# A gated delta-rule recurrence cut into one stream per head pair, each with its own PSUM bank, and emitted in an order that counts more time for VectorE's steps

## The chip, the core and the metric

The kernel runs on one core of one Trainium2 chip. The metric is the device time of one execution in microseconds (us). The engines are named as the profile names them: PE is TensorE (PEld its weight loads), DVE is VectorE, ACT is ScalarE, POOL is GpSimd and SP the engine that issues the DMAs. Each engine works through its own instructions strictly in the order in which they were emitted.

## What is computed

One layer of a hybrid streaming encoder for 2048 prompt rows and 32 sample rows of width 1024: a LayerNorm, one wide input projection, a chunk-band softmax attention (branch A), a gated DeltaNet (branch B), two output projections, a gated merge and a last projection with LayerNorm. Branch B has 8 heads of width 64 and works on chunks of 64 rows. Its core, cut to what matters here, is a scan over the chunks:

```python
def step(s, blk_in):
    q_c, k_c, u_c, w_c, gc_c, qk_c = blk_in
    v_new = u_c - jnp.einsum('bhld,bhde->bhle', w_c, s)
    o_c = (jnp.einsum('bhld,bhde->bhle', q_c * jnp.exp(gc_c)[..., None], s)
           + jnp.einsum('bhij,bhje->bhie', qk_c, v_new))
    g_last = gc_c[..., -1]
    k_dec = k_c * jnp.exp(g_last[..., None] - gc_c)[..., None]
    s = s * jnp.exp(g_last)[..., None, None] + jnp.einsum('bhld,bhle->bhde', k_dec, v_new)
    return s, o_c
s_final, o = lax.scan(step, s0.astype(f32), (qb, kb, u, w, gc, qk))
```

The state `s` of a chunk is needed by the next chunk of the same head, and by no other head.

## The kernel before

The prompt is worked on in two halves of 1024 rows. Each half has a stage for branch B (`phase_b`, here called the first and the second recurrence stage) and one for branch A (`phase_a`); after the second attention stage the branches are merged. The input projections are not a stage of their own. `fetch`, `divide` and `multiply` stream the 49 weight blocks through all stages, and their products (tile `pj`, three f16 passes that stand for one f32 product) are what PE does between the small products of the stage. Which jobs a stage gets is fixed (`ORDER`, `FILL`, `TAIL`): in a recurrence stage they are the blocks of branch B and some gate blocks, and the jobs of the attention stage can begin only when the recurrence stage has ended (`done`), since its buffers take the same memory.

Nothing is scheduled by the tile framework. Python generators emit the instructions: `Flow.run` always steps the generator whose clock is earliest, `Engine.price` puts a cost on each instruction, and `Flow.spend` moves the generator's clock to the end that these costs give. So these clocks are a plan, from which nothing but the order on each engine is left. A `Gate` hands out slots (buffers), a `Mark` is an event.

In a recurrence stage the 8 heads are 4 pairs (`p` 0 to 3, two heads side by side on the 128 partitions), and a half has two blocks of 8 chunks for each pair; the second half ends with one block for the sample rows. For each block `prep` makes the decays, `local`/`system` the chunk products (`k_bd`, `qk_bd`), `solve`/`substitute` the triangular systems on DVE (`sys_t`, `sys_u`), `side` the scaled operands (`q_bd`, `kd_bd`, `v_t`), and `inverse` assembles `u_bd` from the solved parts (`tu`, `z_c`). Then `chain` runs the recurrence over the block, and `tail` normalises its rows (`v_t`), transposes them on PE and stores them.

`chain` (L1255 on) is one generator for all blocks in a row. A chunk has five f32 products of 64 columns, each done in two passes, and four small steps: `xs` = state by `k_bd` (PE), `os` = state by `q_bd` (PE), `r` (DVE, reads `xs`), `ys` = `r` by `u_bd` (PE), `vn` (DVE, reads `ys`), `ds` = `vn` by `kd_bd` (PE), `os` += `vn` by `qk_bd` (PE), the new state (DVE, reads `ds`), and a copy of `os` to `v_t` (ACT). `xs`, `os` and `ys` take turns in three PSUM banks (`a`), `ds` has one of its own (`c`); `a` serves `inverse` and `tail` as well.

```python
yield bank["a"]
xs = pt("a")
PE.matmul(xs[:, 0:HD], k.kb[:, c, :], st, start=True, stop=True)
yield bank["a"]
os_ = pt("a")
PE.matmul(os_[:, 0:HD], k.qb[:, c, :], st, start=True, stop=False)
```

The line number of nearly every instruction in the profile is that of the helper that emits it (L243), so operations are told by their tiles.

Of the kernel before, what the change touches and what calls it, by code (L numbers as in the profile page):

```python
# [11 lines left out]
F32 = mybir.dt.float32  # L12
# [37 lines left out]
HEAD, TAIL = [2, 3], [6, 6]  # L50
AHEAD = 100.0
SPREAD = 20.0
HOP_PE, HOP, HOP_SAME = 0.1, 0.2, 0.12
# [28 lines left out]
class Gate:  # L82
# [169 lines left out]
def trunk(ctx: ExitStack, tc: tile.TileContext, x_p, x_s, cache_k, cache_v, st_conv, st_gdn,  # L252
# [11 lines left out]
    def dma(dst, src, eng=nc.sync):  # L264

        eng.dma_start(dst, src)  # L266
        n = 4
        for k in dst.shape:
            n *= k

        n = max(n, n // (4 * dst.shape[-1]) * 768)
        return flow.transfer("SP" if eng is nc.sync else "S", n)

    def gate(n):
        return Gate(flow, n)

    def mark():
        return Mark(flow)
# [4 lines left out]

    banks = {"pj": 2, "a": 3, "b": 2, "c": 1}
    bank = {k: gate(n) for k, n in banks.items()}

    def pt(tag):

        return psum.tile([P, 512], F32, tag=tag, bufs=banks[tag], name=tag)

# [448 lines left out]
    def phase_b(half):  # L739

        stack = ExitStack()
        bp = stack.enter_context(tc.tile_pool(name=f"bp{half}", bufs=1, reuse_waits="tile"))
        last = half == 1
# [26 lines left out]

        pd = [dram.tile([32, 1024], F32, name=f"sol_p{half}{i}") for i in range(NSIDE)]
        ud = [dram.tile([32, 1024], F32, name=f"sol_u{half}{i}") for i in range(NSIDE)]

# [39 lines left out]
        raw_slots, qk_slots, v_slots = gate(2), gate(NQK), gate(2)  # L813
        par_slots, side_slots, u_slots = gate(NPAR), gate(NSIDE), gate(NSIDE)
        e_slot, tail_slot, p_slots, vt_slots = gate(1), gate(2), gate(NSIDE), gate(NSIDE)
        todo, decays, q_sys = Queue(flow), Queue(flow), Queue(flow)
# [176 lines left out]
        def prep():  # L993
            yield decay_done
            for k in order:
# [23 lines left out]
                yield  # L1019
                k.sc = bp.tile([P, 4, 8], F32, tag="sc", bufs=7, name="sc")  # L1020
                s_k, s_l = (k.sc[:, i, 0:nch] for i in (2, 3))
# [45 lines left out]
        def side(k, ss):  # L1067
# [4 lines left out]
            G.tensor_tensor(out=k.sc[:, 0, 0:nch], in0=ss[:, 1, 0:nch], in1=expo[:, 1, 0:nch], op=ALU.pow)  # L1072
            yield side_slots
            k.qb, k.kdb = q_bd[k.n % NSIDE], kd_bd[k.n % NSIDE]
            for h in range(2):
# [25 lines left out]
            yield from by_token(k.qk[:, 1, :], nch, put_k)  # L1101
            yield vt_slots
            k.v_t = bp.tile([P, 8, HD], F32, tag="v_t", bufs=NSIDE, name="v_t")
            yield bank["b"]
# [16 lines left out]
        def system(k):  # L1121

            nch = k.nch
            n = nch * CH
            yield par_slots
            yield k.qk_ready
            yield k.prep
            yield p_slots
            kb, qkb = k.kb, k.qkb = k_bd[k.n % NPAR], qk_bd[k.n % NPAR]
            p_c = k.p_c = bp.tile([P, 8, HD], F32, tag="p_c", bufs=NSIDE, name="p_c")  # L1130
# [4 lines left out]
            ss = bp.tile([P, 2, 8], F32, tag="ss", bufs=6, name="ss")  # L1135
            k.rr = bp.tile([P, 8], F32, tag="rr", bufs=7, name="rr")
            yield bank["b"]
# [26 lines left out]

            dv = pd[k.n % NSIDE][:].rearrange("(c k) (j i) -> k j c i", k=4, i=32)
            for q in range(4):
# [5 lines left out]
        def solve():  # L1172
            while True:
                k, t = yield from q_sys.get()
                sys_p = bp.tile([P, 32, 32], F32, tag="sys_p", bufs=2, name="sys_p")
                sys_u = bp.tile([P, 8, 32], F32, tag="sys_u", bufs=2, name="sys_u")
                sys_t = bp.tile([P, 8, 32], F32, tag="sys_t", bufs=2, name="sys_t")
                G.memset(sys_u[:], 0.0)
                for g in range(4):
                    G.memset(sys_u[g * 32:(g + 1) * 32].rearrange("p r i -> p (r i)")[:, g::36], 1.0)  # L1180
                yield t
                p0 = pd[k.n % NSIDE][:]
                yield dma(sys_p[:].rearrange("p j i -> p (j i)"),
                          bass.AP(p0.tensor, p0.offset, [[0, 4], [1024, 32], [1, 1024]]))
                yield from substitute(sys_p, sys_u, sys_t)
                for g in range(4):
                    t = dma(ud[k.n % NSIDE][:].rearrange("s (r g i) -> g s r i", g=4, i=32)[g], sys_u[g * 32:(g + 1) * 32])
                flow.start(inverse(k, t))
# [15 lines left out]
        def inverse(k, t):  # L1204

            yield u_slots
            k.ub = u_bd[k.n % NSIDE]
            nch, ub, p_c = k.nch, k.ub, k.p_c
            u0 = ud[k.n % NSIDE][:]
            yield t  # L1210
# [33 lines left out]
            for h in range(2):  # L1244
# [3 lines left out]
                bank["ba"[h]].give()  # L1248
            p_slots.give()
            yield k.side  # L1250
            k.ready.done()


        def chain():
            for k in order:  # L1255
                yield k.ready
                sc, v_t = k.sc, k.v_t
                for c in range(k.nch):
                    st = k.state[c]
                    vc = v_t[:, c if k.p is None else c % 4 * 2 + c // 4, :]  # L1260
                    yield bank["a"]
                    xs = pt("a")
                    PE.matmul(xs[:, 0:HD], k.kb[:, c, :], st, start=True, stop=True)
                    yield bank["a"]
                    os_ = pt("a")
                    PE.matmul(os_[:, 0:HD], k.qb[:, c, :], st, start=True, stop=False)
                    flow.cur.last = None
                    r = bp.tile([P, HD], F32, tag="r", bufs=2, name="r")
                    V.scalar_tensor_tensor(out=r[:], in0=xs[:, 0:HD], scalar=k.negc[:, c:c + 1],
                                           in1=vc, op0=ALU.mult, op1=ALU.add)  # L1270
                    bank["a"].give()
                    yield bank["a"]
                    ys = pt("a")
                    PE.matmul(ys[:, 0:HD], k.ub[:, c, :], r[:], start=True, stop=True)
                    yield
                    vn = bp.tile([P, HD], F32, tag="vn", bufs=2, name="vn")
                    V.tensor_scalar(out=vn[:], in0=ys[:, 0:HD], scalar1=sc[:, 1, c:c + 1], scalar2=None, op0=ALU.mult)
                    bank["a"].give()
                    yield
                    yield bank["c"]  # L1280
                    ds_ = pt("c")
                    PE.matmul(ds_[:, 0:HD], k.kdb[:, c, :], vn[:], start=True, stop=True)
                    PE.matmul(os_[:, 0:HD], k.qkb[:, c, :], vn[:], start=False, stop=True)
                    V.scalar_tensor_tensor(out=st, in0=st, scalar=sc[:, 3, c:c + 1], in1=ds_[:, 0:HD],
                                           op0=ALU.mult, op1=ALU.add)
                    bank["c"].give()

                    S.copy(out=vc, in_=os_[:, 0:HD])
                    bank["a"].give()
                    yield  # L1290
                for g in (par_slots, side_slots, u_slots):
                    g.give()
                flow.start(tail(k))

        def tail(k):
# [43 lines left out]
            else:  # L1339
# [20 lines left out]
                yield t  # L1360
            vt_slots.give()
            if k.p is None:
# [3 lines left out]
            tail_slot.give()  # L1366
            if k is order[-1]:
                done.done()
# [5 lines left out]

        for g in (worker(todo), worker(decays), prep(), local(), solve(), solve(), chain()):
            flow.start(g)
        return stack, make, done


    def phase_a(half):  # L1380
        stack = ExitStack()
        ap = stack.enter_context(tc.tile_pool(name=f"ap{half}", bufs=1, reuse_waits="tile"))
        last = half == 1
# [756 lines left out]

    with tc.tile_pool(name="x0", bufs=1, reuse_waits="tile") as xp:
# [87 lines left out]
```

## Time and profile before

| what | us |
|---|---|
| median of 3 runs (lowest to highest) | 2184.65 (2179.92 to 2190.05) |
| the profiled execution | 2182.41 |
| its span in the profile | 2180.4 |
| PE busy | 2014.9 |
| DVE busy | 1563.9 |
| ACT busy | 1024.8 |
| POOL busy | 636.1 |
| first recurrence stage, about | 47 to 559 |
| first attention stage, about | 559 to 888 |
| second recurrence stage, about | 888 to 1410 |
| second attention stage, about | 1410 to 1795 |
| merge, about | 1795 to 2180 |

A row of instructions names the engine, the operation, the tile written and the tiles read, and the shape. In the table of groups the numbers after the bar are busy us and mean ns of one, and after the second bar the engine's idle us just before these instructions, with the instruction that ended most of it. In the table of windows each engine has its busy us and its number of instructions; PEclk is the granted share of PE's clock. In the timeline a row has its start, its length and, in brackets, the idle time before it and what ended that.

### The profile page before, as it was taken

The numbers are of one execution on the slowest core, as the hardware profiler recorded it, in microseconds if no ns is written. First come the engines' busy times: TensorE is split into PE (matmuls) and PEld (weight loads), VectorE is DVE, ScalarE is ACT, GpSimd is POOL, SyncE is SP. The second block draws the span as 40 slices with busy tenths as digits, with TensorE's granted clock in tenths as the row PEclk, the third lists the DMA queues.
The fourth block names the chain that finished last, engine by engine and source line by source line (L and its number), as shares of the span: only waits on it lengthen the run. The fifth ranks groups of instructions, "written<-read, shape, count | busy, mean of one in ns | idle before, by whom it ended". The sixth has DMA issues, their size and how long they took to land. (4 is left out here: it accounts for less than half of the span.)

```text
span 2180.4 us, 41182 instructions
## 1 busy us (share of the span) xinstructions
PE 2014.9 (92%) x15098; PEld 1441.5 (66%) x15098; DVE 1563.9 (72%) x4700; ACT 1024.8 (47%) x2178; POOL 636.1 (29%) x708
## 2 busy tenths in 40 slices
PE   4898998999899999998999999889999998999998
PEld 4454665666455556666777776667676577998896
DVE  7689878873378677679898877447567577676675
ACT  5654545433476677564443533256666652111110
POOL 6343333232212113333223332310110214443333
PEclk9999999999899999999999999999999999999999
DMA  3233232322213113222223223221221325443331
GB/s 119 71 83 104 76 93 53 90 86 83 72 47 102 47 62 111 66 66 66 72 63 98 66 85 89 85 82 41 70 64 47 117 86 192 135 133 110 116 104 59
DMA packets 181718, 185.99 MB, mean 85 GB/s; under 512 B 73862, under 2 KB 131570, under 8 KB 181516
## 3 DMA queue, kind: packets, MB, share of 16 engines
q1 hardware_dynamic: 181516, 183.36, 28.1%
q8 instruction: 119, 1.95, 0.4%
q14 instruction: 83, 0.68, 0.1%
HBM read 135.91 MB, written 50.53 MB: 86 GB/s over the span
## 5 line engine op out<-in xcount | busy, mean ns | idle before, releaser
L243 PE MATMUL pj<-hi,whi 128*128 128x512 f16 (+2 forms) x1992 | 660.1, 346 | 25.6 <-DVE ql L243 7.4
L243 PE MATMUL pj<-hi,wlo 128*128 128x512 f16 (+2 forms) x1952 | 649.8, 345 | 0.9 <-POOL wlo L243 0.9
L243 PEld LDWEIGHTS <-whi 128*128 128x128 f16 x3984 | 412.7, 105 | 230.8 <-issue 17.9
L243 PE MATMUL pj<-lo,whi 128*128 128x512 f16 (+2 forms) x1992 | 458.6, 342 | 0.0
L243 POOL TENSOR_TENSOR wlo<-wraw,whi 128x512 f16<-128x512 f32 x192 | 228.3, 1190 | 702.3 <-ACT whi L243 454.1
L243 PEld LDWEIGHTS <-wlo 128*128 128x128 f16 x1952 | 205.0, 105 | 124.1 <-issue 24.5
L243 ACT CAST mh<-sg 128x256 fp32r<-128x256 f32 x64 | 26.0, 406 | 283.0 <-DVE sg L243 283.0
L243 DVE TENSOR_TENSOR sys_u<-sys_u,sys_t 128x60 f32<-128x60 f32 (+24 forms) x527 | 135.8, 258 | 18.5 <-DVE sys_t L243 0.2
L243 PE MATMUL a<-ghi,whi 128*128 128x256 f32 (+1 forms) x512 | 133.6, 291 | 7.2 <-DVE sg L243 6.9
L243 ACT ACTIVATE wraw<-wraw,w_scale 128x1024 f32<-128x1024 f32 (+1 forms) x98 | 111.4, 1137 | 56.8 <-DVE w_scale L243 56.3
L243 ACT CAST ph<-b 128x512 f16<-128x512 f32 (+2 forms) x224 | 92.4, 421 | 88.2 <-PE b L243 81.5
L243 PE MATMUL a<-ghi,wlo 128*128 128x256 f32 (+1 forms) x512 | 131.8, 288 | 1.0 <-DVE wlo L243 0.9
L243 ACT CAST whi<-wraw 128x512 f16<-128x512 f32 (+1 forms) x196 | 119.6, 611 | 20.2 <-PE pj L243 17.2
L243 ACT ACTIVATE sb<-sb,mx,unit 128x640 f32<-128x640 f32 (+4 forms) x128 | 109.0, 852 | 39.6 <-DVE mx L243 38.8
L243 DVE TENSOR_TENSOR pl<-b,ph 128x512 f16<-128x512 f32 (+2 forms) x224 | 107.2, 485 | 24.1 <-ACT ph L243 22.9
L243 DVE TENSOR_TENSOR sys_t<-sys_u,sys_p 128x60 f32<-128x60 f32 (+21 forms) x459 | 116.3, 253 | 4.7
L243 ACT COPY v_t<-a 128x64 f32<-128x64 f32 x132 | 27.8, 211 | 194.2 <-PE a L243 185.5
L243 DVE SCALAR_TENSOR_TENSOR acc<-raw,cwT,acc 128x512 f32<-128x512 f32 x144 | 113.4, 787 | 6.0 <-ACT acc L243 5.0
L243 POOL TENSOR_TENSOR w_scale<-w_scale,mhalf 128x1 f32<-128x1 f32 x49 | 30.6, 625 | 297.5 <-DVE w_scale L243 233.7
L243 PE MATMUL b<-ident,sb 128*128 128x128 f32 x560 | 100.9, 281 | 7.7 <-ACT sb L243 2.8
L243 PEld LDWEIGHTS a<-ghi,whi 128*128 128x128 f32 x512 | 99.1, 194 | 9.0 <-DVE sg L243 8.3
L243 PEld LDWEIGHTS a<-ghi,wlo 128*128 128x128 f32 x512 | 98.8, 193 | 1.8 <-DVE wlo L243 1.5
(358 smaller groups left out, 4339.1 us busy)
## 6 DMA issues: line engine op xcount, KB each, us to landing
wraw<-in_w_in SPq DMA_DIRECT2D x192, 256.0 KB
sg<-sig SPq DMA_DIRECT2D x112, 128.0 KB
sig<-sig SPq DMA_DIRECT2D x44, 256.0 KB
sys_p<-sol_p SPq DMA_DIRECT2D x17, 512.0 KB
x<-in_x_p SPq DMA_DIRECT2D x16, 512.0 KB
xt<-in_x_p SPq DMA_DIRECT2D x16, 512.0 KB
out_y_p<-xt SPq DMA_DIRECT2D x16, 512.0 KB
glo<-g SPq DMA_DIRECT2D x14, 512.0 KB
```

The costliest lines, as they stand in the source:

```text
L243: r = f(*a, **k)
```

## The change

`chain` is started once for each pair (and once for the sample rows), with that pair's blocks alone. A block first takes one of two PSUM banks of a new kind `x` and gives it back at its end, so at most two blocks are in the recurrence at a time. All four products of a chunk lie in the block's own bank, in one half of it for even and in the other for odd chunks. The product of the state by `q_bd` moves from behind `xs` to behind `ds`. Behind `r` and behind `vn` the generator's clock is moved on by `SLACK` = 0.5 in the blocks of pairs 0, 1 and 2. The other banks are opened by stage: `a` has three before and in the attention stages and two in a recurrence stage. Since blocks no longer end in a fixed order, buffers are handed out by number (`Places`) in place of the block's number modulo their count; there are more of the small buffers `sc`, `ss`, `rr`, and eight in place of three DRAM tiles for the systems.

```diff
+SLACK = 0.5
+class Places(Gate):
+    def __init__(self, flow, n):
+        super().__init__(flow, n)
+        self.numbers = deque(range(n))
+    def take(self):
+        yield self
+        return self.numbers.popleft()
+    def back(self, i):
+        self.numbers.append(i)
+        self.give()
...
-    banks = {"pj": 2, "a": 3, "b": 2, "c": 1}
+    banks = {"pj": 2, "b": 2}
...
     def phase_b(half):
         stack = ExitStack()
+        open_banks(stack, f"psb{half}", a=2, x=2)
...
+        x_banks = places(2)
+        xb = [pt("x") for _ in range(2)]
...
-        def chain():
-            for k in order:
+        def chain(some):
+            for k in some:
                 yield k.ready
+                xn = yield from x_banks.take()
                 for c in range(k.nch):
...
+                    xs, os_, ys, ds_ = (xb[xn][:, (c % 2 * 4 + i) * HD:(c % 2 * 4 + i + 1) * HD] for i in range(4))
+                    PE.matmul(xs, k.kb[:, c, :], st, start=True, stop=True)
+                    V.scalar_tensor_tensor(out=r[:], in0=xs, scalar=k.negc[:, c:c + 1], in1=vc, op0=ALU.mult, op1=ALU.add)
+                    flow.cur.clock += SLACK * (k.p in (0, 1, 2))
+                    yield
+                    PE.matmul(ys, k.ub[:, c, :], r[:], start=True, stop=True)
+                    yield
+                    V.tensor_scalar(out=vn[:], in0=ys, scalar1=sc[:, 1, c:c + 1], scalar2=None, op0=ALU.mult)
+                    flow.cur.clock += SLACK * (k.p in (0, 1, 2))
+                    yield
+                    PE.matmul(ds_, k.kdb[:, c, :], vn[:], start=True, stop=True)
+                    PE.matmul(os_, k.qb[:, c, :], st, start=True, stop=False)
+                    PE.matmul(os_, k.qkb[:, c, :], vn[:], start=False, stop=True)
+                    V.scalar_tensor_tensor(out=st, in0=st, scalar=sc[:, 3, c:c + 1], in1=ds_, op0=ALU.mult, op1=ALU.add)
+                    S.copy(out=vc, in_=os_)
+                    yield
+                x_banks.back(xn)
...
-        for g in (worker(todo), worker(decays), prep(), local(), solve(), solve(), chain()):
+        for g in (worker(todo), worker(decays), prep(), local(), solve(), solve()):
             flow.start(g)
+        for some in blocks + ([[sample]] if last else []):
+            flow.start(chain(some))
```

The number of instructions of each kind on each engine is the same before and after. What changes is their order, and what some of them wait for. The first place is on PE, in the middle of the first recurrence stage, the third chunk of pair 2's second block, from the product `ys` (by `u_bd`) to `ds` (by `kd_bd`). Before:

```order
L243 MATMUL a_5117<-r_5109,u_bd2_626 128x64 [waits DVE_49]
L243 LDWEIGHTS whi_4711
L243 MATMUL pj_5102<-hi01_149,whi_4711 128x512
L243 LDWEIGHTS wlo_4712
L243 MATMUL pj_5102<-hi01_149,wlo_4712 128x512
L243 MATMUL c_5126<-vn_5120,kd_bd2_620 128x64 [waits DVE_49]
L243 MATMUL a_5107<-vn_5120,qk_bd1_604 128x64
```

The same chunk with the change, again on PE from `ys` to `ds`:

```order
L261 MATMUL x_660<-r_4977,u_bd2_633 128x64 [waits DVE_49]
L261 LDWEIGHTS wlo_4752
L261 MATMUL pj_4987<-hi00_150,wlo_4752 128x512
L261 LDWEIGHTS whi_4751
L261 MATMUL pj_4987<-hi00_150,whi_4751 128x512
L261 LDWEIGHTS wlo_4752 [waits Pool_49]
L261 MATMUL pj_4987<-hi00_150,wlo_4752 128x512
L261 LDWEIGHTS whi_4751
L261 MATMUL pj_4987<-hi00_150,whi_4751 128x512
L261 LDWEIGHTS wlo_4752
L261 MATMUL pj_4987<-hi00_150,wlo_4752 128x512
L261 MATMUL x_660<-vn_5004,kd_bd2_627 128x64 [waits DVE_49]
```

Five projection products now stand where two stood, while DVE makes `vn`. The second place is on PE as well, at the end of the first recurrence stage, in pair 3's second block, the last of the stage. Before, its sixth chunk, from the product by `q_bd` on, reads:

```order
L243 MATMUL a_5951<-state_118,q_bd1_612 128x64
L243 LDWEIGHTS whi_5618
L243 MATMUL pj_5906<-lo01_150,whi_5618 128x512
L243 LDWEIGHTS whi_5618
L243 MATMUL pj_5906<-lo01_150,whi_5618 128x512
L243 MATMUL a_5957<-r_5953,u_bd1_624 128x64 [waits DVE_49,Activation_49]
L243 LDWEIGHTS whi_5618
L243 MATMUL pj_5906<-lo01_150,whi_5618 128x512
L243 LDWEIGHTS whi_5618
L243 MATMUL pj_5906<-lo01_150,whi_5618 128x512
L243 MATMUL c_5963<-vn_5960,kd_bd1_618 128x64 [waits DVE_49]
L243 MATMUL a_5951<-vn_5960,qk_bd3_608 128x64
```

With the change the same block begins, on PE, with the end of its `inverse` (`tu`, `z_c`) and its first two chunks like this, and goes on in this way through all eight:

```order
L261 MATMUL a_5637<-tu_5530,z_c_5622 32x32 [waits Activation_49]
L261 MATMUL a_5637<-tu_5530,z_c_5622 32x32 x7
L261 MATMUL x_660<-state_118,k_bd3_607 128x64
L261 MATMUL x_660<-r_5685,u_bd1_631 128x64 [waits DVE_49,Activation_49]
L261 MATMUL x_660<-vn_5689,kd_bd1_625 128x64 [waits DVE_49]
L261 MATMUL x_660<-state_118,q_bd1_619 128x64
L261 MATMUL x_660<-vn_5689,qk_bd3_615 128x64
L261 MATMUL x_660<-state_118,k_bd3_607 128x64 [waits Activation_49]
L261 MATMUL x_660<-r_5701,u_bd1_631 128x64 [waits DVE_49]
L261 MATMUL x_660<-vn_5704,kd_bd1_625 128x64 [waits DVE_49]
L261 MATMUL x_660<-state_118,q_bd1_619 128x64
L261 MATMUL x_660<-vn_5704,qk_bd3_615 128x64
```

No projection product is left between the steps: the last of the stage now stands ahead of this block's `inverse`, where before it stood behind the block's sixth chunk. The rows show a changed wait, too. The product by `k_bd` that opens a chunk waited for DVE (the new state) and now waits for ACT (the copy of the chunk before), which in turn waits for DVE's new state, since both read the block's one bank; and the new state waits for the product by `qk_bd`, not for the one by `kd_bd`. At the end of the second recurrence stage, on the other hand, 45 projection products of 272 columns stand on PE between the last chunk and the last `tail`'s transposes, where 6 stood before.

More of the change, by code (lines that the diff above doesn't have):

```diff
@@ L275, in gate, with places @@
         return Gate(flow, n)
+    def places(n):
+        return Places(flow, n)
     def mark():
@@ L282, in trunk, with open_banks @@
     dram = ctx.enter_context(tc.tile_pool(name="dram", bufs=1, space=DRAM))
-    banks = {"pj": 2, "a": 3, "b": 2, "c": 1}
+    banks = {"pj": 2, "b": 2}
     bank = {k: gate(n) for k, n in banks.items()}
+    bank_pool = {k: psum for k in banks}
+    def open_banks(stack, name, **more):
+        pool = stack.enter_context(tc.tile_pool(name=name, bufs=1, space=PSUM, reuse_waits="tile"))
+        for k, n in more.items():
+            banks[k], bank[k], bank_pool[k] = n, gate(n), pool
     def pt(tag):
-        return psum.tile([P, 512], F32, tag=tag, bufs=banks[tag], name=tag)
+        return bank_pool[tag].tile([P, 512], F32, tag=tag, bufs=banks[tag], name=tag)
     g_dram = [dram.tile([NP, P, T], F32, name=f"g{b}") for b in range(2)]
@@ L769, in phase_b @@
         q_bd, kd_bd, u_bd = (diag(n, NSIDE) for n in ("q_bd", "kd_bd", "u_bd"))
-        pd = [dram.tile([32, 1024], F32, name=f"sol_p{half}{i}") for i in range(NSIDE)]
-        ud = [dram.tile([32, 1024], F32, name=f"sol_u{half}{i}") for i in range(NSIDE)]
+        pd = [dram.tile([32, 1024], F32, name=f"sol_p{half}{i}") for i in range(2 * NP)]
+        ud = [dram.tile([32, 1024], F32, name=f"sol_u{half}{i}") for i in range(2 * NP)]
+        p_cs, v_ts = ([bp.tile([P, 8, HD], F32, name=f"{x}{i}") for i in range(NSIDE)] for x in ("p_c", "v_t"))
         col = bp.tile([P, 2, NP, nch_all], F32, name="col")
@@ L1072, in side @@
             G.tensor_tensor(out=k.sc[:, 0, 0:nch], in0=ss[:, 1, 0:nch], in1=expo[:, 1, 0:nch], op=ALU.pow)
-            yield side_slots
-            k.qb, k.kdb = q_bd[k.n % NSIDE], kd_bd[k.n % NSIDE]
+            k.sn = yield from side_slots.take()
+            k.qb, k.kdb = q_bd[k.sn], kd_bd[k.sn]
             for h in range(2):
@@ L1101, in side @@
             yield from by_token(k.qk[:, 1, :], nch, put_k)
-            yield vt_slots
-            k.v_t = bp.tile([P, 8, HD], F32, tag="v_t", bufs=NSIDE, name="v_t")
+            k.vn = yield from vt_slots.take()
+            k.v_t = v_ts[k.vn]
             yield bank["b"]
@@ L1124, in system @@
             n = nch * CH
-            yield par_slots
+            k.par = yield from par_slots.take()
             yield k.qk_ready
             yield k.prep
-            yield p_slots
-            kb, qkb = k.kb, k.qkb = k_bd[k.n % NPAR], qk_bd[k.n % NPAR]
-            p_c = k.p_c = bp.tile([P, 8, HD], F32, tag="p_c", bufs=NSIDE, name="p_c")
+            k.pn = yield from p_slots.take()
+            kb, qkb = k.kb, k.qkb = k_bd[k.par], qk_bd[k.par]
+            p_c = k.p_c = p_cs[k.pn]
             qk, e_in, sc = k.qk, k.e_in, k.sc
@@ L1204, in inverse @@
         def inverse(k, t):
-            yield u_slots
-            k.ub = u_bd[k.n % NSIDE]
+            k.un = yield from u_slots.take()
+            k.ub = u_bd[k.un]
             nch, ub, p_c = k.nch, k.ub, k.p_c
-            u0 = ud[k.n % NSIDE][:]
+            u0 = ud[k.n % (2 * NP)][:]
             yield t
@@ L1260, in chain @@
                     vc = v_t[:, c if k.p is None else c % 4 * 2 + c // 4, :]
[L1261 to L1268, printed above, removed]
@@ L1279, in chain @@
                     yield
[L1280 to L1288, printed above, removed]
@@ L1360, in tail @@
                 yield t
-            vt_slots.give()
+            vt_slots.back(k.vn)
             if k.p is None:
@@ L1366, in tail @@
             tail_slot.give()
-            if k is order[-1]:
+            left[0] -= 1
+            if not left[0]:
                 done.done()
```

41 lines of the change are left out of this document (19 added, 22 removed).

## The prediction

> **What bounds the kernel now.** First the page: the span, the share of each engine, the 40 slices.
>
> ```profile
> span 2180.4 us, 41182 instructions
> ...
> PE   4898998999899999998999999889999998999998
> ...
> DVE  7689878873378677679898877447567577676675
> ...
> PEclk9999999999899999999999999999999999999999
> ```
>
> PE is at eight or nine tenths in all slices but the first, and DVE reaches eight or nine only in recurrence slices. PE sets the time, so a microsecond is gained only where PE idles or runs at a lower clock. The table of windows shows how much that is, for the two recurrence stages and for a dense stretch of the first (start:end, length, busy us by engine with instructions, PEclk, DMA).
>
> ```profile
> core 0: us, PE busy (x) PEld busy (x) DVE busy (x) ACT busy (x) POOL busy (x), PEclk, DMA share, GB/s
> 47.00:559.00 512.00, 471.40 (x3199) 297.12 (x3198) 390.29 (x1279) 247.48 (x473) 167.96 (x212) 0.95 0.29 82
> 888.00:1410.00 522.00, 481.48 (x3936) 353.97 (x3934) 402.88 (x1302) 238.77 (x507) 155.91 (x217) 0.96 0.28 77
> 207.00:281.00 74.00, 67.43 (x479) 43.47 (x478) 66.21 (x223) 38.80 (x78) 23.20 (x30) 0.98 0.28 80
> 464.00:472.00 8.00, 4.78 (x22) 3.35 (x21) 3.22 (x16) 0.21 (x1) 0.74 (x1) 0.79 0.49 145
> ```
>
> PE idles 40.6 us in the first stage (512 − 471.4) and 40.5 in the second. The clock takes 512 × 0.05 = 26 and 522 × 0.04 = 21 us more. Next, the groups: idle time ahead of the chain's products, and how often it occurred by the list of waits (total, times, longest).
>
> ```profile
> L243 PE MATMUL a<-r,u_bd 128*128 128x64 f32 x264 | 49.0, 268 | 23.4 <-DVE r L243 18.4 <-DVE sys_t L243 3.8 <-ACT zb L243 0.8
> L243 PE MATMUL c<-vn,kd_bd 128*128 128x64 f32 x264 | 53.1, 284 | 14.3 <-DVE vn L243 10.9 <-DVE w_scale L243 3.0
> L243 PE MATMUL a<-state,k_bd 128*128 128x64 f32 x256 | 44.8, 258 | 1.4 <-DVE state L243 1.1
> PE a L243 <- DVE r L243: 18.4, 20, 2.7
> PE c L243 <- DVE vn L243: 10.9, 15, 3.2
> ```
>
> The chain's waits are 23.4 + 14.3 + 1.4 = 39.1 us, 48% of the 81.1. They are few and long: 132 chunks give 20 waits for `r` and 15 for `vn`. In the other chunks the projection products cover DVE's step. This is what the change can reach.
>
> **The change, part by part.** The counts of instructions do not change, so every term is a wait or a clock. Counts of products are read from the two orders.
>
> *More cover behind `r` and `vn`.* In the 48 chunks of pairs 0 to 2 of the first stage, `xs` to `ys` goes from a median of 3 products of 512 columns to 5, but the product by `q_bd`, worth about one, leaves that place; by the mean it is one more. `ys` to `ds` goes from 5.3 to 6.7 in the mean, and chunks with two or fewer from 12 to 1. In the second stage the median goes from 4 to 5.9, the thin ones from 11 to 4. What a product covers is the spacing of two:
>
> ```profile
> 513.29 0.38 PE L243 MATMUL pj<-hi,whi 128*128 128x512 f16 x1
> ...
> 513.51 0.38 PE L243 MATMUL pj<-hi,wlo 128*128 128x512 f16 x1
> ```
>
> 0.22 us. A wait can shrink by no more than the cover added to it: 20 × 0.21 = 4.2 and 15 × 0.43 (two products) = 6.5, together **−10.7**. Bounds: nothing, if DVE merely comes later where it is dense, and −26, two thirds of 39.1, if the thin chunks are those that wait.
>
> *The clock.* The window 464:472 has PEclk 0.79, around one wait of 3.2 us for `vn`, the longest of the list. The idle time that the chain causes is 48%; put down by that share it causes 22 of the 47 us, and 10.7 of 39.1, 27%, goes: **−6** (0 to −15).
>
> By the Trainium skill, "TensorE: Matmul & The Clock Gate", section "Part 1: The HAM clock gate (the "warmup" mystery)", the clock halves after an idle window of about 3.4 us and comes back after a busy one. The 0.79 above, beside a wait of 3.2 us, goes with the rule. By it only the one or two longest waits would pay here, and this term would be near −2 instead of −6.
>
> *End of the second recurrence stage.* The last `tail`'s transposes wait for POOL:
>
> ```profile
> 1401.53 0.28 PE L243 MATMUL pj<-hi,whi 128*128 128x272 f16 x1
> ...
> 1401.65 0.28 PE L243 MATMUL pj<-hi,wlo 128*128 128x272 f16 x1
> ...
> 1402.97 0.86 PE L243 MATMUL pj<-lo,whi 128*128 128x272 f16 x6
> ...
> 1409.96 1.60 PE L243 MATMUL a<-ident,v_t 64*64 64x64 f32 x16 [6.13 <-POOL v_t L243]
> 1403.10:1410.00 6.90, 0.77 (x8) 0.42 (x5) 3.31 (x10) 3.08 (x6) 3.93 (x5) 0.79 0.24 58
> ```
>
> These products stand 0.12 apart. With 45 in place of 6 the cover is 5.4 instead of 0.7 us, so 4.7 of 6.13 goes; with the low clock of this window (0.79 over 6.9 us is 1.4, and some behind it) **−6.5** (−4 to −8).
>
> *End of the first recurrence stage.* Here the change takes cover away: pair 3's second block has no product between its steps.
>
> ```profile
> 538.80:546.60 7.80, 7.80 (x49) 5.27 (x48) 2.10 (x8) 1.32 (x4) 0.00 (x0) 1.00 0.50 137
> 545.77 1.03 PE L243 MATMUL pj<-lo,whi 128*128 128x512 f16 x4
> ...
> 514.25 0.69 PE L243 MATMUL b<-tu_t,p_c 32*32 32x32 f32 x16
> ...
> 517.41 1.15 ACT L243 ACTIVATE wraw<-wraw,w_scale 128x1024 f32<-128x1024 f32 x1 [1.12 <-DVE w_scale L243]
> ...
> 518.59 0.62 ACT L243 CAST whi<-wraw 128x512 f16<-128x512 f32 x1
> L243 ACT COPY u_bd<-b 32x256 f32<-32x256 f32 (+1 forms) x17 | 6.0, 352 | 9.7 <-PE b L243 9.7
> ```
>
> PE is full up to 546.6, and the stage's last product ends at 546.8. Six chunks of five products (0.2 each where PE is full: 6.0) and the inverse's three steps (0.69 each: 2.1) stood ahead of it and now stand behind, so it ends at 538.7. From there to the first `ys` it takes the inverse's way through ACT, where a weight block's scale and cast stand between `z_c` and `u_bd` in the new order: from 514.25 to the cast's end at 519.21 and two copies of 0.36, 5.7 in all. That is 544.4. Then eight bare chunks. One that was already bare:
>
> ```profile
> 546.63 0.33 PE L243 MATMUL a<-state,k_bd 128*128 128x64 f32 x2
> ...
> 547.00 0.28 DVE L243 SCALAR_TENSOR_TENSOR r<-a,negc,v_t 128x64 f32<-128x64 f32 x1 [0.97 <-PE a L243]
> 547.43 0.41 PE L243 MATMUL a<-r,u_bd 128*128 128x64 f32 x2 [0.25 <-DVE r L243]
> ...
> 548.33 0.41 PE L243 MATMUL c<-vn,kd_bd 128*128 128x64 f32 x2
> 548.58 0.39 PE L243 MATMUL a<-vn,qk_bd 128*128 128x64 f32 x2
> 548.78 0.28 DVE L243 SCALAR_TENSOR_TENSOR state<-state,sc,c 128x64 f32<-128x64 f32 x1 [0.62 <-PE c L243]
> 549.00 0.21 ACT L243 COPY v_t<-a 128x64 f32<-128x64 f32 x1 [0.40 <-PE a L243]
> 549.11 0.43 PE L243 MATMUL a<-state,k_bd 128*128 128x64 f32 x2
> ...
> 550.82 0.69 PE L243 MATMUL c<-vn,kd_bd 128*128 128x64 f32 x2 [0.40 <-DVE vn L243]
> 551.30 0.64 PE L243 MATMUL a<-vn,qk_bd 128*128 128x64 f32 x2
> 551.98 0.21 ACT L243 COPY v_t<-a 128x64 f32<-128x64 f32 x1
> 546.60:558.30 11.70, 4.06 (x23) 3.21 (x22) 4.80 (x18) 5.05 (x9) 5.54 (x5) 0.66 0.24 81
> ```
>
> It took 2.48 us (546.63 to 549.11). Now the state waits for two more products (548.58 − 548.33 = 0.25 and as much less a little: 0.46), and the next `xs` for the copy behind the state (0.21 + 0.04): 3.19. Eight of them less the 0.8 up to the first `ys` are 24.7 and end at 569.1. At the low clock the product by `kd_bd` takes 0.69, not 0.41, and the next follows after 0.48, not 0.25: 3 × 0.28 + 2 × 0.23 = 1.3 more in a chunk, so 35.1, to 579.5. Before, the chain ended at 552.2. That is +16.9 or +27.3. The window above has PEclk 0.66 with bare chunks, between the two clocks, so I take the middle: **+22**. The wait for the last `tail` behind it stays.
>
> The copy's place in that chunk has a reason in a page. By the Trainium skill, "PSUM — Partial Sum Buffer", section "PSUM bank collisions raise a hardware error ⚠️", two engines may not touch one bank's quadrant at once, reads by ScalarE and VectorE included. The rows agree as far as they go: the state at 548.78 to 549.06 and the copy from 549.00 overlap, in two banks. Without this the copy's 0.25 in eight chunks would be out, +20 instead of +22.
>
> *Pair 3 and the shared bank elsewhere.* The filled chunks have four products (0.88) between the one by `qk_bd` and the next `xs`, which covers the new 0.46 + 0.25. Pair 3 has no `SLACK`: `xs` to `ys` falls from 3 products to 1 in the first stage and from 2.65 to 2.06 in the second. A bare step needs 0.47 (547.43 − 546.96, the end of `xs`), so about 0.25 stays open in the 8 chunks not counted yet, 2.0, and up to 2.1 in the second stage's 16: **+3** (0 to 5; not below, as cover only shrinks).
>
> Sum: −10.7 − 6 − 6.5 + 22 + 3 = +1.8 on the profiled execution's 2182.41 (span 2180.4, about 2 around it): 2184. The median shown, 2184.65, is 2.2 above that execution, within the spread of its runs.
>
> **Rivals.** *The thin chunks were the ones that waited* (faster). For it: few, long waits, and 23 thin places become 5. Against it: the longest, up to 3.2 us, exceed what any five products (1.1) cover. With half of the 39.1 gone, −20, the clock −11, −6.5, +17 (the full clock's end) and +3: 2165. With two thirds, −26, −15: 2155.
>
> *DVE is the bound where it is dense* (slower). In 207:281 DVE is busy 66.21 of 74 us, 89%, nearly PE's share (67.43). There an earlier product only makes PE wait at another place, now at `xs` for ACT's copy, which stands behind the state on DVE. Then the chain's term is −3, the clock 0, the second stage's end −4, its bare chunks at the low clock +27, pair 3 +4: 2206. It decides from where waits and clock together give less than 27 + 4 − 4 − 11 = 16 us.
>
> *Bare chunks keep the clock* (between). If, by the waits, only the long ones cost clock, the end is +17 and the sum −3 or so: 2179. This is inside the first forecast's reach, and is what the clock page named above would make of the stage's end, whose gaps are each below 1 us; the 0.66 measured there speaks against it.
>
> *The streams do not run two at a time.* In the order, of 16 blocks four neighbours overlap, by two or three chunks in the first stage and by one at most in the second. So no term rests on two streams filling each other's waits; the result is the forecast's own.
>
> **How the numbers follow.** A measurement of this kernel can tell about 0.5%, 11 us, from no change: below 2173.7 is faster, above 2195.6 slower. Forecast with the clock rival 0.41, thin chunks 0.34, dense DVE 0.25, and the same three as signs. The likeliest case's own range is 2174 to 2195. For 8 in 10 the range takes in most of both rivals: 2157 to 2206, leaving about 0.1 at either side.
>
> **What would show it.** Right: idle time ahead of the product by `u_bd` falls from 23.4 to about 19, ahead of that by `kd_bd` from 14.3 to 8; behind the last product of the first stage eight chunks 3.2 to 4.5 us apart, with PEclk near 0.6, and its end some 14 us later against the stage's start than before, net of the saved waits; the wait of 6.13 at about 1.4; recurrence PEclk 0.95 to 0.96. Thin chunks: both groups below half, recurrence PEclk 0.97 or more. Dense DVE: idle time returns ahead of the product by `k_bd`, released by ACT's copy, well over 1.4 us. It would be wrong altogether if the saved time came back in the attention stages, whose work is in the same order, or if transfers for the solves came later through SP's shifted places: then waits of DVE for `sys_p` would grow.

## The result and the profile after

| | before | changed |
|---|---|---|
| median of 20 runs, us | 2184.57 | 2192.49 |
| lowest to highest | 2173.78 to 2193.59 | 2186.75 to 2199.25 |
| ratio to before (95% interval) | | 1.0033 (1.0022 to 1.0044) |
| profiled execution, its span | 2182.41, 2180.4 | 2190.96, 2189.1 |

The changed kernel is 0.33% slower. The forecast was 2184 and "no change that can be told". The time lies in the range and within 0.5%, but it moved to the slow side, and two errors in the sum, +16 us in one stage and −8 in the other, partly cancelled. One of the eight executions of run 6 below took 2388.50 us at a granted clock of 0.841 and is left out of its median. Every window and group of a run is of one execution. First the page of the changed kernel, the lines that were shown of before:

```profile
span 2189.1 us, 41031 instructions
...
PE   4898989998899999898999999999999998999998
...
DVE  7689879863368667668988787447567477676676
...
PEclk9999999998799999999999999999999999999999
```

In PEclk the tenth and eleventh slices (about 490 to 600 us, the end of the first recurrence stage) now have 8 and 7, where only the eleventh had an 8 before; the dip in DVE's row stood there before, too. The table of windows, cut at the same events as before: the first stage from its first chunk to its last projection product, from there to the last `tail`, then to the second stage's first chunk, and the second stage to its last `tail`. Before:

```profile
212.40:546.80 334.40, 312.48 (x2260) 210.96 (x2258) 252.86 (x925) 148.50 (x308) 100.42 (x122) 0.95 0.29 81
546.80:558.30 11.50, 3.86 (x22) 3.04 (x21) 4.80 (x18) 5.05 (x9) 5.54 (x5) 0.65 0.24 82
558.30:1042.40 484.10, 455.63 (x3427) 284.29 (x3428) 345.25 (x1063) 305.45 (x607) 127.06 (x161) 0.97 0.23 71
1042.40:1410.00 367.60, 340.86 (x2870) 258.90 (x2868) 285.55 (x1019) 153.74 (x351) 106.88 (x136) 0.96 0.29 79
```

And of the changed kernel, with the second stage's last 5.4 us apart as well:

```profile
213.80:522.60 308.80, 293.14 (x2136) 191.90 (x2135) 247.33 (x903) 144.05 (x298) 101.66 (x122) 0.99 0.31 85
522.60:566.40 43.80, 25.53 (x146) 20.83 (x146) 10.09 (x39) 7.92 (x19) 5.54 (x5) 0.55 0.13 42
566.40:1052.00 485.60, 457.18 (x3427) 285.13 (x3428) 344.77 (x1063) 306.03 (x607) 127.02 (x161) 0.97 0.23 71
1052.00:1422.40 370.40, 347.53 (x2863) 258.55 (x2861) 288.23 (x1019) 151.18 (x348) 103.84 (x133) 0.96 0.29 78
1417.00:1422.40 5.40, 5.40 (x45) 4.21 (x43) 1.43 (x7) 2.73 (x5) 1.62 (x2) 1.00 0.42 119
```

The differences add up to the 8.7 us between the spans: +1.4 before the first chunk, −25.6, +32.3, +1.5, +2.8, and −3.7 behind the second stage (766.7 against 770.4). So the first stage got 6.7 us longer, where the terms gave about +15 (+22, and half of −10.7, −6 and +3), and the second 2.8 longer, where they gave about −13 (−6.5 and the other halves). The groups of the chain's products, with their idle time, and the releasers in the list of waits:

```profile
L261 PE MATMUL x<-r,u_bd 128*128 128x64 f32 x264 | 51.2, 278 | 11.5 <-DVE r L261 7.7 <-DVE sys_t L261 1.8 <-ACT u_bd L261 1.7
L261 PE MATMUL x<-vn,kd_bd 128*128 128x64 f32 x264 | 52.4, 282 | 17.0 <-DVE vn L261 16.8
L261 PE MATMUL x<-state,k_bd 128*128 128x64 f32 x256 | 50.8, 282 | 18.0 <-ACT v_t L261 17.9
L261 PE MATMUL x<-state,q_bd 128*128 128x64 f32 x256 | 52.4, 288 | 0.0
L261 PE MATMUL a<-ident,v_t 128*128 128x128 f32 (+1 forms) x80 | 12.1, 281 | 5.8 <-POOL v_t L261 5.8
PE x L261 <- ACT v_t L261: 17.9, 23, 4.6
```

The wait for `r` fell by half, the one for `vn` rose from 14.3, and 18.0 us stand ahead of `k_bd`, where 1.4 stood. Next the start of pair 3's last block on PE in the timeline, and one of its bare chunks:

```profile
525.86 0.43 PE L261 MATMUL x<-state,k_bd 128*128 128x64 f32 x2
527.97 0.69 PE L261 MATMUL x<-r,u_bd 128*128 128x64 f32 x2 [1.68 <-ACT u_bd L261]
...
535.49 0.69 PE L261 MATMUL x<-state,k_bd 128*128 128x64 f32 x2 [0.62 <-ACT v_t L261]
536.56 0.69 PE L261 MATMUL x<-r,u_bd 128*128 128x64 f32 x2 [0.38 <-DVE r L261]
537.63 0.69 PE L261 MATMUL x<-vn,kd_bd 128*128 128x64 f32 x2 [0.38 <-DVE vn L261]
538.11 0.63 PE L261 MATMUL x<-state,q_bd 128*128 128x64 f32 x2
538.54 0.63 PE L261 MATMUL x<-vn,qk_bd 128*128 128x64 f32 x2
539.79 0.69 PE L261 MATMUL x<-state,k_bd 128*128 128x64 f32 x2 [0.62 <-ACT v_t L261]
```

A chunk takes 4.30 us, with every product at the low clock's 0.63 to 0.69 (forecast: 3.19 to 4.49). That end came as forecast; the rest had to be found by taking the change apart.

### The profile page after: what moved, and what is told of

Its sections match the earlier page's. It is cut to its first block, busy times and chain, and to the rows that moved or that the text cites. A ratio compares the mean times of both kernels' runs of the same rounds, so it can differ in the third digit from the quotient of the medians.

```text
span 2189.1 us, 41031 instructions
## 1 busy us (share of the span) xinstructions
PE 2020.0 (92%) x15098; PEld 1437.2 (66%) x15098; DVE 1563.3 (71%) x4700; ACT 1023.7 (47%) x2178; POOL 633.8 (29%) x708
## 5 line engine op out<-in xcount | busy, mean ns | idle before, releaser
L261 PEld LDWEIGHTS <-whi 128*128 128x128 f16 x3984 | 405.1, 103 | 233.5 <-issue 11.6
L261 PE MATMUL pj<-lo,whi 128*128 128x512 f16 (+2 forms) x1992 | 447.3, 341 | 0.0
L261 ACT COPY v_t<-x 128x64 f32<-128x64 f32 x132 | 28.0, 212 | 285.3 <-DVE state L261 276.2
L261 ACT CAST whi<-wraw 128x512 f16<-128x512 f32 (+1 forms) x196 | 119.5, 611 | 22.6 <-PE pj L261 19.6
```

The lines of the kernel that those rows point to most:

```text
L261: r = f(*a, **k)
```

## The experiments

All times are medians; ratios are against the kernel before on the same chip, with 95% intervals. Runs 1 to 8 and runs 9 to 12 are of two chips, so between these the ratios are compared.

**1. The bare end filled.**

```diff
-HEAD, TAIL = [2, 3], [6, 6]
+HEAD, TAIL = [2, 3], [8, 6]
```

> The changed kernel with TAIL of the first half 8 in place of 6: two more gate jobs (96 projection products) are worked off in the first recurrence stage instead of behind the first attention stage, so pair 3's last block has 2 to 6 products between its steps again and 13 behind it; everything ahead of that block is in the same order as in the changed kernel. Theory A (the bare last block is the price of the change): of the 43.9 us from the stage's last product to the last tail, 18.3 of idle time falls to about 3 and 19.6 of half clock to about 1; part of it is given back where the two jobs are missing later. Some 20 to 33 us faster than the changed kernel, about 2165. Rival B (the bare block only moves the same idle time out of other places, since the attention stage needs those jobs as cover): within 5 us of the changed kernel, 2188 to 2197, with the idle time of the first attention stage (28.4 us) up by 20 or more.

Measured: 2173.12, ratio 0.9937 (0.9918 to 0.9956). Its windows, the first stage to its last product, from there to the last `tail`, and the attention stage:

```profile
213.70:557.00 343.30, 326.33 (x2377) 211.12 (x2375) 258.00 (x946) 157.06 (x325) 107.30 (x129) 1.00 0.31 85
557.00:560.60 3.60, 0.42 (x4) 0.30 (x3) 1.04 (x7) 2.51 (x4) 3.15 (x3) 1.00 0.20 73
560.60:1032.50 471.90, 438.99 (x3327) 277.64 (x3328) 341.19 (x1053) 298.71 (x596) 120.17 (x157) 0.96 0.23 70
```

43.8 us became 3.6. The first stage is 5.7 us shorter than in the changed kernel (346.9 against 352.6) with 96 products (21 us at 0.22) more in it. The attention stage without them is only 13.7 shorter, so 7 us were given back there. A holds: the bare block is worth some 20 us net.

**2. and 3. One stream, and `os` in a bank of its own.**

```diff
-        x_banks = places(2)
+        x_banks = places(1)
```

```diff
-    ... = (xb[xn][:, ...] for i in range(4))
+    ... = (xb[i == 1][:, ...] for i in range(4))
```

The second kernel has both edits.

> The changed kernel with one bank x handed out, so one block at a time; SLACK, the shared bank and the place of the product by q_bd stay. In its order no product is left behind the last chunk of the second recurrence stage. Theory A (the two streams matter only for the cover at that stage's end): about 6 to 9 us slower than the changed kernel, near 2200, with the wait of 6 us ahead of the last transposes back, and the groups ahead of u_bd, kd_bd and k_bd about as in the changed kernel (11.5, 17.0, 18.0). Rival B (two streams share DVE and PSUM and hinder each other): faster than the changed kernel, 2180 to 2188, with the waits ahead of k_bd and kd_bd down by a third.

> As the run with one stream, instruction for instruction in the same order, but the output os of a chunk lies in the second bank x, so the new state waits for kd_bd's product alone and the next xs for the state alone, not for ACT's copy. To be compared with the run with one stream. Theory A (the shared bank puts PE behind DVE and ACT, 18.0 us of idle time ahead of k_bd): the idle time ahead of k_bd falls from about 18 to 4 or less, and each of the eight bare chunks at the first stage's end becomes 0.7 to 1.2 us shorter; 12 to 20 us faster than with the shared bank. Rival B (DVE is late for other reasons): the idle time goes to u_bd and kd_bd instead, and only the bare chunks gain, 6 to 9 us.

Measured: 2198.68 (1.0057, 1.0036 to 1.0079) and 2188.58 (1.0010, 0.9995 to 1.0025). With one stream 7.1 us of idle time stand ahead of the last transposes again: A, and the wait behind the forecast's −6.5 is there (the intervals of this time and of the changed kernel's overlap). The bank in the same order is worth 10 us. The groups ahead of `k_bd`, first with one stream, then with `os` in its own bank, each for the whole execution and for the bare stretch (57.5 us long, then 50.9), and the second stages of the two runs and of run 4:

```profile
L261 PE MATMUL x<-state,k_bd 128*128 128x64 f32 x256 | 52.2, 287 | 16.5 <-ACT v_t L261 16.0
L261 PE MATMUL x<-state,k_bd 128*128 128x64 f32 x22 | 7.5, 447 | 5.6 <-ACT v_t L261 5.6
...
L261 PE MATMUL x<-state,k_bd 128*128 128x64 f32 x256 | 50.1, 280 | 10.8 <-DVE state L261 10.7
L261 PE MATMUL x<-state,k_bd 128*128 128x64 f32 x22 | 7.4, 440 | 0.0
...
1054.20:1429.50 375.30, 348.16 (x2870) 257.32 (x2868) 287.29 (x1019) 153.16 (x351) 105.20 (x136) 0.96 0.29 78
1046.00:1419.10 373.10, 346.11 (x2869) 259.89 (x2867) 285.47 (x1020) 153.79 (x352) 105.09 (x135) 0.96 0.29 78
1034.40:1409.10 374.70, 349.41 (x2850) 252.70 (x2848) 284.41 (x1019) 150.15 (x348) 104.24 (x134) 0.97 0.28 77
```

6.6 of the 10 us lie in the bare stretch, 2.2 in the second stage. All the idle time that is saved ahead of `k_bd` is saved in the bare stretch (5.6 to nothing). In the filled chunks 10.9 us become 10.8, and only the name of the releaser changes, from ACT's copy to DVE's state: there DVE is late, whatever the bank. This is nearer to B.

**4. Without `SLACK`.**

```diff
-SLACK = 0.5
+SLACK = 0.0
```

> The changed kernel with SLACK = 0: two streams, the shared bank and the place of the product by q_bd stay. In its order the first stage's last block has products between its steps and 25 behind it, but xs to ys has a median of 2 products instead of 4. Theory A (SLACK is what shortened the waits for r and took the half clock out of the first stage, at the price of the bare block): the idle time ahead of u_bd is 25 us or more instead of 11.5, the half clock of the first stage's filled part comes back (3.4 to 12 or more), the bare block's 38 us of idle time and half clock go; in sum 5 to 15 us faster than the changed kernel, about 2182. Rival B (SLACK costs nothing at the end, since cover missing there is cover used before): within 4 us of the changed kernel or slower.

Measured: 2188.82, ratio 1.0018 (1.0002 to 1.0034). The group ahead of `u_bd` is back at 22.6, and the bare block is gone, but the sum gains 3.7 us only, within B's bound. So where the end is filled (run 1), `SLACK` is worth about 16 us, near the forecast's 10.7 + 6, though a few of them may be the two jobs that run 1 moved (run 7). What the run leaves is the real question: with no bare end and the second stage's end covered, this kernel should beat the one before by some 17 us, and it is 4 slower. Some 20 us are lost elsewhere.

**5. and 6. `SLACK` = 0, `os` in a bank `a` (same order as run 4), then also the product by `q_bd` back behind `xs`.**

```diff
+                    yield bank["a"]
+                    os_ = pt("a")[:, 0:HD]
...
                     S.copy(out=vc, in_=os_)
+                    bank["a"].give()
```

```diff
                     PE.matmul(xs, k.kb[:, c, :], st, start=True, stop=True)
+                    yield bank["a"]
+                    os_ = pt("a")[:, 0:HD]
+                    PE.matmul(os_, k.qb[:, c, :], st, start=True, stop=False)
+                    flow.cur.last = None
...
                     PE.matmul(ds_, k.kdb[:, c, :], vn[:], start=True, stop=True)
-                    PE.matmul(os_, k.qb[:, c, :], st, start=True, stop=False)
```

> As the run with SLACK = 0 (two streams, product by q_bd behind ds), instruction for instruction in the same order, but os lies in a bank a of its own, so that the copy on ACT and the two products of os no longer stand between ds and the next xs. To be compared with the run with SLACK = 0 (2188.8). It asks where the 10 us are that streams, bank and moved product cost together and that the prediction had at 3. Theory A (where chunks have products between their steps, the shared bank costs next to nothing, as the 4.3 us of idle time ahead of k_bd there say): 0 to 4 us faster. Rival B (the shared bank costs most of the 10 us): 7 to 12 us faster.

> As the run before it, with the product by q_bd back behind xs: the streams alone are left of the change (SLACK = 0, os in a bank a). In its order xs to ys has a median of 3 products again and two or fewer in 13 places instead of 61; the first stage's last two chunks are bare as in the kernel before, which costs some 10 us against the run with SLACK = 0. Theory A (the moved product takes cover from r and, as the third f32 product in a row, PE time): the filled part of both recurrence stages becomes 8 to 12 us shorter, idle time ahead of u_bd at most the 23.4 of the kernel before, mean slot of a product by q_bd and k_bd back at 0.09 us; in sum about 2178 to 2184. Rival B (its place costs nothing): the filled part stays within 3 us and the sum is about 2195.

Measured: 2182.16 (0.9992, 0.9977 to 1.0007) and 2166.81 (0.9923, 0.9892 to 0.9953). The bank: 0.26% by the ratios, with intervals that overlap, between A and B; not settled by this pair. The second stage got no shorter by it (374.7 us in run 4, 376.1 in run 5). The product's place: 15 us, although two bare chunks come back with it. The second stage, with and without the moved product:

```profile
1034.40:1410.50 376.10, 349.13 (x2850) 256.55 (x2848) 285.38 (x1019) 150.32 (x348) 104.25 (x134) 0.96 0.29 77
1036.60:1389.20 352.60, 337.25 (x2839) 255.85 (x2837) 282.67 (x1019) 150.16 (x346) 103.69 (x134) 0.96 0.31 81
```

23.5 us: 11.6 of idle time (27.0 against 15.4) and 11.9 of PE's busy time, with 11 products fewer (under 2 us) and the same clock. A, and more than it said. The moved product changes the planned order of other instructions too, so this is the price of its place together with the order that comes with it.

**7. Control: the kernel before with TAIL 8.**

> The kernel before, with TAIL of the first half 8 in place of 6, as control for the run of the changed kernel with 8: its last two chunks get products and the last tail 37 products ahead of it. Theory A (the bare end costs what its idle time and half clock say, 7.7 + 4.0 us): 8 to 12 us faster than before, 2173 to 2177; the changed kernel with 8 (2173.1) is then no faster than this, and SLACK pays no more than bank and moved product cost. Rival B (the two jobs are missing as cover behind the first attention stage): within 4 us of before.

Measured: 2179.61, ratio 0.9980 (0.9966 to 0.9995), nearer to B. The bare end goes (345.0 us from the first chunk to the last `tail` against 345.9, with 51 products more, 11 us), but the attention stage without them takes 483.5 against 484.1: it gives all of it back. So most of run 1's gain (19 us against 4 here) is not that of two jobs moved; it is the change's own bare block.

**8. `SLACK`, TAIL 9, both other edits undone.**

> The changed kernel with SLACK, TAIL 9, os in a bank a of its own and the product by q_bd behind xs: SLACK and two streams without what else the change brought. Theory A (SLACK is worth some 15 us when the end is filled, and bank and moved product cost some 10): 2160 to 2168, idle time ahead of u_bd, kd_bd and k_bd together under 25 us (14 less than before). Rival B (DVE is late where it is dense, and the waits move as they did in the second stage): 2170 to 2177, with the three groups above 33 us.

Measured: 2164.58, ratio 0.9905 (0.9881 to 0.9929): A's time, but the three groups sum to 30.0, between the two. Three jobs look too many to take from the attention stage: it lasts 473.1 us, 12.5 less for 144 products, some 31 us of work.

**9. The moved product alone, in the kernel before.** Its edit is the second of run 6 the other way round, on the single stream.

> The kernel before with one part of the change alone: the product by q_bd stands behind ds (one stream, os in a bank a, no SLACK). In its order xs to ys falls from a median of 3 products to 2, with two or fewer in 56 places instead of 14, and both recurrence stages now end with 23 to 25 products behind the last chunk. Theory A (the moved product was cover for r): the filled parts of the two stages become 12 to 20 us longer, idle time ahead of u_bd at or above 23.4 and the mean slot of a product by u_bd above 0.15 us (0.127 before), while the covered ends give 14 to 18 back; in sum within 5 us of before. Rival B (the moved product costs nothing, the loss of the other runs lay with the streams): only the gain at the ends is left, 12 to 18 us faster than before, about 2169.

Measured: 2174.22, ratio 0.9954 (0.9937 to 0.9972): between the two. Its groups ahead of `u_bd` and of the moved product, then the first stage (to its last product, then to the last `tail`) and the second:

```profile
L243 PE MATMUL a<-r,u_bd 128*128 128x64 f32 x264 | 53.4, 284 | 26.6 <-DVE r L243 17.3 <-DVE sys_t L243 3.2 <-DVE ms L243 1.7
L243 PE MATMUL a<-state,q_bd 128*128 128x64 f32 x256 | 50.5, 280 | 0.0
212.70:543.90 331.20, 313.29 (x2277) 202.07 (x2275) 256.09 (x936) 148.81 (x311) 102.52 (x124) 0.98 0.29 82
543.90:545.40 1.50, 0.23 (x2) 0.23 (x3) 0.00 (x0) 1.43 (x3) 0.57 (x1) 1.00 0.00 0
1025.60:1399.10 373.50, 345.02 (x2851) 254.44 (x2849) 291.55 (x1020) 150.68 (x348) 104.34 (x134) 0.97 0.28 77
```

The cost is there: the second stage takes 373.5 against 367.6 with 19 products fewer, and the products by `u_bd` (284 against 268 ns) and by `q_bd` (280 against 258) lie longer on PE. So is a gain: both stages' ends are covered in the order that comes with it (1.5 us in place of 11.5, and no wait of 6). It also shows that the covered end of the second stage comes from either edit, not from the streams alone.

**10. and 11. Run 1 with `os` in a bank `a`, then also with the product back.**

> The run with TAIL 8 again (SLACK, two streams, product by q_bd behind ds), with os in a bank a of its own; in its order fewer products, 6 instead of 25, stand behind the last chunk of the second stage. Theory A (with SLACK the waits stand ahead of k_bd, and half of them are the copy's): idle time ahead of k_bd falls from 14.8 to 6 to 10, released by DVE's state; filled parts 5 to 8 us shorter, some 3 of it lost at the second stage's end; in sum 2 to 6 us faster than 2173. Rival B (DVE's lateness sets it, the bank only names another releaser): the filled parts within 2 us, the sum slower by 2 to 4.

> As the run before it, with the product by q_bd back behind xs; in its order six chunks at the first stage's end are bare, and 14 and 8 products stand at the second stage's end. Theory A (SLACK has already given back the cover that the moved product took): the second recurrence stage up to its last tail is 5 to 12 us shorter, the first stage's filled part per product about the same, its end 18 to 24 us longer; in sum 8 to 15 us slower than the run before it. Rival B (the moved product costs 15 us whatever SLACK is): both filled parts shorter by 7 or more each, the sum within 5 us.

Measured: 2167.35 (0.9917, 0.9887 to 0.9948) and 2165.29 (0.9912, 0.9886 to 0.9939). The second stage of run 1 and of run 10, then run 11's bare end and its second stage:

```profile
1032.50:1406.00 373.50, 350.45 (x2864) 260.47 (x2862) 288.75 (x1019) 151.22 (x348) 103.65 (x133) 0.95 0.29 78
...
1031.20:1394.80 363.60, 340.58 (x2870) 254.85 (x2868) 285.48 (x1019) 153.50 (x351) 102.85 (x135) 0.97 0.30 80
...
555.40:574.90 19.50, 11.21 (x47) 9.16 (x46) 5.99 (x25) 5.50 (x12) 5.51 (x5) 0.60 0.22 68
1050.40:1395.60 345.20, 329.61 (x2860) 251.62 (x2860) 285.36 (x1027) 151.53 (x347) 102.17 (x133) 0.99 0.31 82
```

Run 10's stage is 9.9 us shorter, the greater part by the clock (0.95 to 0.97), and idle time ahead of `k_bd` falls from 14.8 to 9.8, released by the state: A, though the two intervals of the whole time overlap. But a chunk now waits for a bank `a` in the plan, and PE's order in that stage is another one than in run 1, so the 9.9 are not the bank's alone. The product gives another 18.4: 7.4 of idle time (23.0 against 15.6), about 7 by the clock (0.97 to 0.99), the rest busy time. The six bare chunks that come with its order (19.5 us) hide this in the sum. B for the second stage; in the first stage's filled part (341.3 and 343.3) nothing is gained.

**12. The streams alone (run 6) with `SLACK` in the second half only.**

```diff
-                    flow.cur.clock += SLACK * (k.p in (0, 1, 2))
+                    flow.cur.clock += SLACK * (last and k.p in (0, 1, 2))
```

> The streams alone (os in a bank a, product by q_bd behind xs, TAIL 6), with SLACK in the second half only, where no bare block follows from it. Theory A (in the second stage SLACK is worth about 10 us, 347.0 + 5.7 against 333.9 + 9.1 in the two runs that have it and don't): 8 to 12 us faster than the streams alone (2167.2), about 2157; that beats both kernels by 1.2%. Rival B (those 10 us were the chance of one profile's clock): within 4 us of 2167.

Measured: 2154.25, ratio 0.9862 (0.9833 to 0.9891), 13 us below run 6. The second stage:

```profile
1036.80:1381.60 344.80, 328.06 (x2860) 250.46 (x2859) 285.49 (x1027) 151.55 (x347) 102.13 (x133) 0.99 0.31 83
```

The stage is 7.8 us shorter than in run 6, and again at a clock of 0.99: A. PE's order in it is that of run 11, and of run 8, where it took 343.0 us. This beats both kernels: 1.4% below the one before, 1.7% below the changed one.

## Why the prediction was wrong

**The step that failed** is the one headed "Pair 3 and the shared bank elsewhere", +3 (0 to 5). It held that the filled chunks' four products cover the longer way from `ds` to the next `xs`, and the step on `r` and `vn` counted the product by `q_bd` as "about one" lost product of cover. In the second stage the moved product and the shared bank together cost about 25 us, where the term had half of 3: 370.4 us in the changed kernel (373.5 in run 1, in the same order), 345.2 in run 11 (344.8 and 343.0 in runs 12 and 8), with nearly the same number of products. Most of it is the product's place: 23.5 from run 5 to 6, 18.4 from run 10 to 11, and about 11 in run 9 (5.9 more, although a wait of about 5 is covered at its end). For the shared bank no price is shown in the filled chunks: in the same order it was worth 2.2 us (run 2 to 3) and −1.4 (run 4 to 5), and the 9.9 from run 1 to 10 come with another order.

The lines say where the 25 us lie. Idle time is 22.9 against 15.6, 7 us. The clock takes 370.4 × 0.04 = 15 against 345.2 × 0.01 = 3, 11 us. About 6 are left within PE's busy time. Two things were overlooked. The moved product was the only cover that every chunk brought with it, between `xs` and `ys`, whatever the projections did. And idle time understates short waits: projection products follow each other every 0.22 us while each row lasts 0.38, so up to 0.16 us of a wait lies inside the row of the product ahead and counts as busy. The rows of the product itself are longer in its new place, behind other f32 products, as well (`q_bd` 280 ns in run 5, 254 in run 6). How the 6 us divide between the two, and that the lower clock follows from the waits, is not shown.

**More cover behind `r` and `vn`, −10.7.** Forecast 39.1 to 28.4. Measured 11.5 + 17.0 + 18.0 = 46.5; eight bare chunks hold 11.7 of this (0.38, 0.38 and 0.62 each, 1.68 and no wait for `k_bd` in the first), so 34.8 in the filled ones, −4. `r` lost far more than forecast (23.4 to about 7), `vn` nothing, and most of it came back ahead of `k_bd`: the mechanism and the sign of the rival "DVE is the bound where it is dense", given 0.25, though not its time. Where the copy that this rival put in the way was taken out in the same order (run 3), the wait in the filled chunks stayed.

**The clock, −6.** In the first stage's filled part PEclk went from 0.95 to 0.99 (334.4 × 0.05 = 17 against 308.8 × 0.01 = 3), in the second it stayed at 0.96: −14 instead of −6, all of it in the first stage, where the forecast had taken it from both.

**End of the second stage, −6.5.** Right: PE is busy 5.40 of 5.40 us at full clock ahead of the last transposes, where 6.13 were idle; the forecast had left 1.4 of them.

**End of the first stage, +22.** Right in size and way: 43.8 against 11.5 us, less the 8.1 of work that moved behind, is +24. The chunk took 4.30 us. That +22 fitted was in part luck: it was the middle between two clocks, and the clock was low from the first product by `u_bd` on, for which the step gave +27.

By the Trainium skill, "TensorE: Matmul & The Clock Gate", section "Part 1: The HAM clock gate (the "warmup" mystery)", the clock halves after an idle window of about 3.4 us. In this stretch PEclk is 0.55 over 43.8 us, with PE busy 25.53 of them. The longest gap on PE ahead of the first slow product is 1.68 us, and between the chunks none is longer than 0.62, so the trace does not agree. The rival built on the rule (bare chunks keep the clock, 2179) is refuted.

**Rivals.** "The streams do not run two at a time" said that no term rests on them. Run 6 has the streams and little else and is 0.8% faster than before, though with the moved product the kernel with one stream (2174.2) is faster than the one with two (2182.2, run 5). Why the two edits work against each other was not found.

**The sum** came within 0.4% by luck: the second stage's miss (+16 us) met a first stage whose waits and clock went further than forecast (−8).

## What to carry to other kernels

Before moving an operation out of a dependent chain, count what it covered there: a small product between two dependent steps is cover in every iteration, and the independent work around it is not. Read short waits from PE's busy time too, since its rows overlap and swallow them. And an order that makes one stretch denser has taken its filler from another: look at the end of the stage for the bare stretch, and test it by giving filler back there (here 20 us).

## What was not expected of the hardware

The longest wait of the changed kernel's chain, 4.60 us ahead of `k_bd`, is put down to ACT's copy. The timeline of all engines at that place:

```profile
322.38 0.24 DVE L261 TENSOR_SCALAR sys_t<-sys_p,sys_u 128x31 f32<-128x31 f32 x1 [5.05 <-DMA sys_p<-sol_p]
...
322.88 0.28 DVE L261 SCALAR_TENSOR_TENSOR state<-state,sc,x 128x64 f32<-128x64 f32 x1
...
323.19 0.21 ACT L261 COPY v_t<-x 128x64 f32<-128x64 f32 x1 [6.49 <-DVE state L261]
...
323.46 0.69 PE L261 MATMUL x<-state,k_bd 128*128 128x64 f32 x2 [4.60 <-ACT v_t L261]
```

DVE was not busy: it stood for 5.05 us at the first step of another block's solve, whose input was still on its way by DMA, and the new state was queued behind. The 3.22 us for `vn` in the kernel before (464.1) have the same cause:

```profile
466.58 0.24 DVE L243 TENSOR_SCALAR sys_t<-sys_p,sys_u 128x31 f32<-128x31 f32 x1 [3.60 <-DMA sys_p<-sol_p]
```

Neither more cover of a microsecond nor a lighter DVE can take these away; an earlier DMA, or a solve emitted later, might, which was not tried. In sum the change did not make these waits of DVE grow, which the prediction had named as a way to be wrong: total, times and longest, before and after.

```profile
DVE sys_t L243 <- DMA sys_p<-sol_p: 15.5, 7, 3.6
DVE sys_t L261 <- DMA sys_p<-sol_p: 9.5, 4, 5.1
```
